# The down projection of a ConvFFN as seven block products in place of eight

## The chip, the core and the metric

The kernel runs on one core of a Trainium2 chip. The metric is device time in microseconds (us). The kernel before takes 1240.32 us, the median of three runs (1239.63 to 1242.1).

## What is computed

One inference step of a decoder layer: a pooling mixer and a Mamba-2 mixer (first 700 us, not touched), their merge, and a ConvFFN over 512 prompt tokens, 64 sample tokens and 16 meta tokens. The change lies in the last lines:

```python
hn2 = rmsnorm(x, norm2_w)
up, ffn_new = causal_dwconv(hn2 @ w_up, ffn_buf, ffn_conv_w, ffn_conv_b)
x = x + (silu(up[..., :D_FF]) * up[..., D_FF:]) @ w_down    # D_MODEL 1024, D_FF 2816
```

After it come a last rmsnorm and the outputs. All data are float32.

## The kernel before, in words

Features lie on the 128 partitions, tokens on the free axis. D_FF is 22 blocks of 128 (gate blocks, j = 0 to 21), D_MODEL 8 blocks (m = 0 to 7). The down projection works on 576 tokens, in two halves of 288.

**A product in three matmuls.** Each float32 operand is split into a high part (a copy in the `F32R` type) and a low part (the rest). `mm3` (lines 117 to 121) multiplies low weight by high activation, high by high, and high weight by low activation, so one block product costs three matmuls, each with its own weight load.

**Units.** A `Unit` (lines 125 to 173) is one output block. `split` takes raw weights from `load_w` (lines 87 to 103: a DMA on SyncE's queue into one of two `wr` buffers, at most two blocks remembered) and splits them: ScalarE copies the high part (line 113), VectorE subtracts for the low part (line 114), into one of two buffers `wh` and `wl`. `product` issues the matmuls, `finish` calls the unit's `post`. `run` (lines 175 to 196) goes through a list of units and splits two units ahead: after unit i's product it splits unit i+2, whose `wh` and `wl` are those that unit i has just read. Outside a block scheduled by hand at the start, the framework orders each engine's instructions ahead of time, and may take a later one that is ready before an earlier one that waits.

**Up projection.** `ff_units` gives a gate unit and a value unit for each j, 48 matmuls each. Both posts call `ffn_conv` (lines 1105 to 1122): VectorE takes the result out of PSUM with three multiplications by the norm (lines 1110 to 1112), ScalarE and VectorE convolve (1118, 1120). `gate_post` applies tanh and a VectorE step (1132, 1133). `val_post` multiplies gate by value (1143), then ScalarE and GpSimd split the product (1147, 1148).

**Down projection.** `down_units` (line 1215) makes one unit per m: first over gate blocks 0 to 11, in two pieces of 6, with 72 matmuls a unit, then, after the other up units, over 12 to 21 with 60 a unit. `down_post` (line 1173) adds the PSUM result to the running sum `x2`. In the last stretch `out_block` (lines 1179 to 1190) transposes a finished block on TensorE, with a square and sum on ScalarE (1189) and a multiplication on VectorE (1190) per tile, and `out_half` (1194 to 1213) scales and stores.

**Buffers.** PSUM has 3 banks under `mm_tile` and 5 under `px_tile`. The pools that matter are `slot` (9), `big` (20), `ext` (3), `acc` (3) and `tmp` (3).

## Time and profile before

| | us |
|---|---|
| median of three runs | 1240.32 |
| the profiled execution | 1240.06 |
| its span, first to last instruction | 1238.3 |
| TensorE matmuls busy | 1215.4 (9148 instructions) |
| VectorE busy | 781.2 |
| ScalarE busy | 557.0 |
| GpSimd busy | 166.4 |

The profile is of one execution. Busy time counts an instruction from its start to its end; matmuls overlap one another, so a busy TensorE is read from the distance of their starts. In the rows PE is TensorE, PEld its weight loads, DVE VectorE, ACT ScalarE, POOL GpSimd, SP SyncE; L114 is line 114. An operand `mm` or `px` lies in PSUM, all others in SBUF.

### The profile page before, as it was taken

How to read it: one execution, taken by the hardware profiler on the slowest of the kernel's cores; microseconds unless marked ns; L12 is line 12 of the kernel's file. 1: busy time of each engine (PE TensorE's matmuls, PEld its weight loads, DVE VectorE, ACT ScalarE, POOL GpSimd, SP SyncE). 2: the span in 40 equal slices, each digit the busy share in tenths (PEclk: the TensorE clock that was granted, in tenths of full speed). 3: DMA queues.
4: the chain of work that ended last, by engine and by line, in shares of the span. 5: the costliest groups of instructions: out<-in, count | busy, mean ns of one | idle time of the engine just before them, and what ended most of it. 6: DMA issues, size and time to landing. Idle time of an engine off the chain costs nothing.

```text
span 1238.3 us, 22581 instructions
## 1 busy us (share of the span) xinstructions
PE 1215.4 (98%) x9148; PEld 1175.7 (95%) x9148; DVE 781.2 (63%) x1372; ACT 557.0 (45%) x1164; POOL 166.4 (13%) x325
## 2 busy tenths in 40 slices
PE   8999999999999999999999999999999999999996
...
PEclk9999999999999999999999999999999999999999
...
GB/s 186 109 76 125 116 89 179 195 179 47 188 83 150 146 120 174 166 128 175 155 146 100 154 149 76 69 69 103 100 71 64 91 86 103 68 69 81 114 75 77
DMA packets 174456, 143.99 MB, mean 116 GB/s; under 512 B 11630, under 2 KB 163854, under 8 KB 174345
## 3 DMA queue, kind: packets, MB, share of 16 engines
...
q10 hardware_dynamic: 384, 0.16, 0.0%
...
## 4 chain that ended last, share of the span: by engine, by line
PE 88%; DMA 4%; DVE 3%; ACT 3%; issue 1%; SPq 1%; ACTq 0%; DVEq 0%
PE mm L119 26%; PE mm L121 26%; PE mm L120 26%; DMA t<-in_state_ssm_dram 3%; PE px L742 1%; PE px L764 1%; PE px L773 1%; DMA t<-in_x_prompt_dram 1%; DVE acc L642 1%; PE px L119 1%; ACT t L852 1%; ACT t L714 1%; PE px L121 1%; PE px L120 1%; PE px L800 1%
## 5 line engine op out<-in xcount | busy, mean ns | idle before, releaser
L119 PE MATMUL mm<-s,wl 128*128 128x288 f32 (+5 forms) x2528 | 757.1, 299 | 1.4 <-ACT s L297 0.9
L120 PE MATMUL mm<-s,wh 128*128 128x288 f32 (+5 forms) x2528 | 752.4, 298 | 0.0
L121 PE MATMUL mm<-s,wh 128*128 128x288 f32 (+5 forms) x2272 | 678.1, 298 | 0.0
L119 PEld LDWEIGHTS mm<-s,wl 128*128 128x128 f32 (+1 forms) x2528 | 476.6, 189 | 10.0 <-issue 6.3
L120 PEld LDWEIGHTS mm<-s,wh 128*128 128x128 f32 (+1 forms) x2528 | 476.6, 189 | 2.7 <-issue 2.4
L121 PEld LDWEIGHTS mm<-s,wh 128*128 128x128 f32 (+1 forms) x2272 | 427.7, 188 | 3.8 <-issue 3.4
L114 DVE TENSOR_TENSOR wl<-wr,wh 128x1024 fp32r<-128x1024 f32 (+2 forms) x165 | 199.3, 1208 | 175.6 <-ACT wh L113 175.1
L113 ACT ACTIVATE wh<-wr 128x1024 fp32r<-128x1024 f32 (+2 forms) x165 | 170.5, 1033 | 233.5 <-PE mm L121 185.5
L121 PE MATMUL mm<-t,wh 128*128 128x290 f32 (+1 forms) x256 | 76.0, 297 | 0.0
L1120 DVE SCALAR_TENSOR_TENSOR acc<-ext,ffT,acc 128x592 f32<-128x592 f32 x88 | 74.2, 844 | 1.7 <-ACT acc L1118 0.2
L642 DVE SCALAR_TENSOR_TENSOR acc<-ext,scT,acc 128x616 f32<-128x616 f32 x72 | 64.0, 889 | 0.8 <-ACT acc L640 0.2
L714 ACT ACTIVATE t<-t,TK 128x128 f32<-128x128 f32 (+1 forms) x160 | 48.5, 384 | 19.4 <-DVE t L712 19.0
L915 POOL TENSOR_TENSOR sqs<-sqs,acc 128x578 f32<-128x578 f32 x19 | 33.4, 1758 | 132.8 <-ACT acc L914 103.3
L121 PEld LDWEIGHTS mm<-t,wh 128*128 128x128 f32 x256 | 48.2, 188 | 0.0
L852 ACT ACTIVATE t<-t,spr 128x128 f32<-128x128 f32 x128 | 40.9, 393 | 12.6 <-PE px L800 12.4
L1147 ACT ACTIVATE s<-ext 128x512 fp32r<-128x512 f32 (+1 forms) x44 | 17.1, 436 | 64.3 <-DVE ext L1143 64.3
L1111 DVE TENSOR_TENSOR ext<-mm,t 128x224 f32<-128x224 f32 x43 | 16.8, 391 | 40.9 <-PE mm L121 40.8
L1148 POOL TENSOR_TENSOR s<-ext,s 128x512 fp32r<-128x512 f32 (+1 forms) x44 | 37.3, 868 | 34.8 <-ACT s L1147 34.8
L1173 DVE TENSOR_TENSOR t<-t,mm 128x288 f32<-128x288 f32 (+2 forms) x30 | 13.6, 452 | 44.5 <-PE mm L121 44.2
L783 POOL TENSOR_TENSOR s<-s,tmp 128x256 f32<-128x256 f32 (+1 forms) x32 | 30.2, 962 | 81.6 <-DVE tmp L777 81.6
L1118 ACT ACTIVATE acc<-ext,ffT 128x592 f32<-128x592 f32 x44 | 38.2, 870 | 1.6 <-DVE ext L1112 1.6
L1114 POOL COPY t<-ext 128x18 f32<-128x18 f32 x44 | 11.4, 259 | 202.6 <-DVE ext L1112 202.5
(290 smaller groups left out, 1274.4 us busy)
## 6 DMA issues: line engine op xcount, KB each, us to landing
...
```

The source lines that it names most:

```text
L113: S.activation(wh[:, :kb, :n], wr, AF.Copy)
L114: V.tensor_tensor(wl[:, :kb, :n], wr, f(wh[:, :kb, :n]), ALU.subtract)
L119: PE.matmul(o, wl[:, k, :m], hi[:, a:b], start=first, stop=False)
L120: PE.matmul(o, wh[:, k, :m], hi[:, a:b], start=False, stop=False)
L121: PE.matmul(o, wh[:, k, :m], lo[:, a:b], start=False, stop=last)
L642: V.scalar_tensor_tensor(acc[:, 0:616], ext[:, k:k + 616], scT[:, kb, 24 + k:25 + k], acc[:, 0:616], op0=ALU.mult, op1=ALU.add)
L714: S.activation(seg[:q, h, :q], seg[:q, h, :q], AF.Exp, scale=-1.0, bias=sums_[:, h:h + 1])
L852: S.activation(v[:, b], v[:, b], AF.Copy, scale=elS[:, 4 * u + 2 * i + b, 4 * g + j:4 * g + j + 1])
L915: G.tensor_tensor(sums[key], sums[key], t[:, :NA], ALU.add)
L1118: S.activation(acc[:, 0:w], ext[:, 0:w], AF.Identity, scale=ffT[:, kb, 16:17], bias=ffT[:, kb, 19:20])
L1120: V.scalar_tensor_tensor(acc[:, 0:w], ext[:, k:k + w], ffT[:, kb, 16 + k:17 + k], acc[:, 0:w], op0=ALU.mult, op1=ALU.add)
L1148: G.tensor_tensor(l, a, f(h), ALU.subtract)
```

## The change

Weights and activations are cut into 2 by 2 blocks: pairs of gate blocks (p = j // 2) against the two blocks of 128 outputs of a column pair (mp) and the two token halves. Seven products of sums and differences replace the eight block products. `Parts` forms the weight sums with four GpSimd additions for each mp and phase; `val_post` forms the activation sums and splits them; `Two` is a unit of two products, each of 3n matmuls of 288 columns for n pairs of gate blocks, and `seven_post` distributes each result to the running sums. A set of seven has eleven VectorE additions and one ScalarE copy behind it.

The order becomes: up units of j 0 to 7, the gate unit of 8, four sets over p 0 to 3, the other up units to j 15, with the gate unit of 16 ahead of four sets over p 4 to 7, the up units to 21, then one set over p 8 and 9, two plain units over blocks 20 and 21, two sets over p 8 to 10, and two plain units (m 6 and 7) over blocks 16 to 21. The output blocks 0 to 3 come between the last sets, 4 and 5 after the first half of m 6. The tile that holds the norm, `rs2`, moves from a `slot` to the tile `sqs`; that hunk is left out here, and empty lines too.

```diff
@@ -171,6 +171,80 @@
             else:
                 self.post(self.pss)
             due[:0] = [fn() for fn in now]
+    SEVEN = (("S3", "T3"), ("A11", "B11"), ("S2", "N2"), ("S1", "N1"), ("A22", "T4"), ("S4", "B22"), ("A12", "B21"))
+    class Parts:
+        def __init__(self, key, nxt):
+            self.key, self.nxt, self.of = key, nxt, None
+        def get(self, name):
+            if self.of is None:
+                wr, n = load_w(*self.key), self.key[2]
+                a11, a12 = wr[:, 0:n:2, 0:128], wr[:, 1:n:2, 0:128]
+                a21, a22 = wr[:, 0:n:2, 128:256], wr[:, 1:n:2, 128:256]
+                s1, s2, s4 = (tmp_tile((128, 4, 128))[:, :n // 2, :] for _ in range(3))
+                G.tensor_tensor(s1, a21, a22, ALU.add)
+                G.tensor_tensor(a21, a11, a21, ALU.add)
+                G.tensor_tensor(s2, s1, a11, ALU.add)
+                G.tensor_tensor(s4, s2, a12, ALU.add)
+                self.of = dict(A11=a11, A12=a12, A22=a22, S1=s1, S2=s2, S3=a21, S4=s4)
+                if self.nxt:
+                    load_w(*self.nxt)
+            return self.of[name]
+    class Two(Unit):
+        def __init__(self, prods):
+            Unit.__init__(self, None, 0, None, None, None, None)
+            self.prods = prods
+        def split(self):
+            if self.ws is None:
+                self.ws = []
+                wh = wp.tile([128, 2, 4, 128], F32R, tag="wh", bufs=WBUFS, name=nm("wh"))
+                wl = wp.tile([128, 2, 4, 128], F32R, tag="wl", bufs=WBUFS, name=nm("wl"))
+                for i, (parts, name, *_) in enumerate(self.prods):
+                    src = parts.get(name)
+                    n = src.shape[1]
+                    S.activation(wh[:, i, :n], src, AF.Copy)
+                    V.tensor_tensor(wl[:, i, :n], src, f(wh[:, i, :n]), ALU.subtract)
+                    self.ws.append(((wh[:, i], wl[:, i]), n))
+        def product(self, halves=None, piece=None):
+            for (_, _, acts, post), (w, n) in zip(self.prods, self.ws):
+                ps = px_tile()
+                for k in range(n):
+                    act = acts(k)
+                    n2 = act[0].shape[1]
+                    mm3(ps[:, :n2], w, k, 128, act, 0, n2, k == 0, k == n - 1)
+                post(ps)
+        def finish(self):
+            for fn in due:
+                fn()
+            due.clear()
+            now = pend[:]
+            pend.clear()
+            due[:0] = [fn() for fn in now]
+    def seven_units(src, k0, kb, mps, acts, post, after=None):
+        keys = [(src, k0, kb, ((256 * mp, 256),)) for mp in mps]
+        prods = []
+        for i, (mp, key) in enumerate(zip(mps, keys)):
+            parts = Parts(key, keys[i + 1] if i + 1 < len(keys) else after)
+            prods += [(parts, w, lambda k, x=x: acts(k)[x], lambda ps, mp=mp, w=w: post(mp, w, ps)) for w, x in SEVEN]
+        return [Two(prods[i:i + 2]) for i in range(0, len(prods), 2)]
     def run(seq, nxt_units=()):
...
     gates = {}
-    gh, gl = [], []
     def gate_post(j, pss):
         ext, acc, w = ffn_conv(j, pss)
@@ -1133,19 +1208,69 @@
         V.scalar_tensor_tensor(ext[:, 0:w], ext[:, 0:w], 1.0, acc[:, 0:w], op0=ALU.add, op1=ALU.mult)
         gates[j] = ext
+    NH = NY // 2
+    gB, quad = {}, {}
+    def split_g(hi, lo, src, eng):
+        S.activation(hi, src, AF.Copy)
+        eng.tensor_tensor(lo, src, f(hi), ALU.subtract)
     def val_post(j, pss):
-        if j % 2 == 0:
-            gh.extend(pairs(2, F32R))
-            gl.extend(pairs(2, F32R))
         _, acc, w = ffn_conv(NF + j, pss)
-        t = gates.pop(j)
-        for a, b in zip(parts(t), parts(acc)):
-            V.tensor_tensor(a, a, b, ALU.mult)
-        hi, lo = blk(gh, j)[:, :NY], blk(gl, j)[:, :NY]
-        for a, h, l in zip(parts(t), (hi[:, 0:NP], hi[:, NP:].rearrange("p (b j) -> p b j", b=NB)),
-                           (lo[:, 0:NP], lo[:, NP:].rearrange("p (b j) -> p b j", b=NB))):
-            S.activation(h, a, AF.Copy)
-            G.tensor_tensor(l, a, f(h), ALU.subtract)
+        t, p, e = gates.pop(j), j // 2, j % 2
+        if e == 0:
+            quad[p] = slot([128, 4, NH])
+        qd = quad[p]
+        g = qd[:, 2 * e:2 * e + 2].rearrange("p h t -> p (h t)")
+        for o, a, b in zip((g[:, 0:NP], g[:, NP:].rearrange("p (b j) -> p b j", b=NB)), parts(t), parts(acc)):
+            V.tensor_tensor(o, a, b, ALU.mult)
+        lastp = p >= 8
+        if e == 0:
+            if lastp:
+                gB[p] = [big([128, 4, NH], F32R) for _ in range(4)]
+                split_g(gB[p][0][:, 0:2], gB[p][1][:, 0:2], qd[:, 0:2], G)
+            else:
+                new = slot if p % 4 == 3 else big
+                gB[p] = [new([128, 4, NH], F32R), new([128, 4, NH], F32R), big([128, 4, NH], F32R),
+                         gB[p - 1][3] if p % 2 else big([128, 4, NH], F32R)]
+                split_g(gB[p][2][:, 0], gB[p][2][:, 2], qd[:, 0], G)
+            return
+        del quad[p]
+        n1, n2 = t[:, 0:NH], t[:, NH:2 * NH]
+        t3, t4 = (acc[:, 0:NH], acc[:, NH:2 * NH]) if lastp else (qd[:, 1], acc[:, 0:NH])
+        o = 2 if lastp else 0
+        if lastp:
+            split_g(gB[p][0][:, 2:4], gB[p][1][:, 2:4], qd[:, 2:4], G)
+        else:
+            split_g(gB[p][0][:, 0:2], gB[p][1][:, 0:2], qd[:, 2:4], G)
+        V.tensor_tensor(n1, qd[:, 0], qd[:, 1], ALU.subtract)
+        V.scalar_tensor_tensor(n2, n1, -1.0, qd[:, 3], op0=ALU.mult, op1=ALU.subtract)
+        V.tensor_tensor(t3, qd[:, 3], qd[:, 1], ALU.subtract)
+        V.scalar_tensor_tensor(t4, n2, -1.0, qd[:, 2], op0=ALU.mult, op1=ALU.subtract)
+        ns = t[:, 0:2 * NH].rearrange("p (h t) -> p h t", h=2)
+        if lastp:
+            split_g(gB[p][2][:, 0:2], gB[p][3][:, 0:2], ns, V)
+            split_g(gB[p][2][:, 2:4], gB[p][3][:, 2:4], acc[:, 0:2 * NH].rearrange("p (h t) -> p h t", h=2), V)
+        else:
+            split_g(gB[p][0][:, 2:4], gB[p][1][:, 2:4], ns, V)
+            split_g(gB[p][2][:, 1], gB[p][2][:, 3], t3, V)
+            i = 2 * (p % 2)
+            split_g(gB[p][3][:, i], gB[p][3][:, i + 1], t4, V)
+    def g_ops(p):
+        a, b, c, d = gB[p]
+        if p >= 8:
+            at = dict(B11=(a, b, 0), B21=(a, b, 2), B22=(a, b, 3), N1=(c, d, 0), N2=(c, d, 1), T3=(c, d, 2), T4=(c, d, 3))
+            return {k: (h[:, i], l[:, i]) for k, (h, l, i) in at.items()}
+        i = 2 * (p % 2)
+        return dict(B21=(a[:, 0], b[:, 0]), B22=(a[:, 1], b[:, 1]), N1=(a[:, 2], b[:, 2]), N2=(a[:, 3], b[:, 3]),
+                    B11=(c[:, 0], c[:, 2]), T3=(c[:, 1], c[:, 3]), T4=(d[:, i], d[:, i + 1]))
+    def g_blk(j):
+        a, b = (x.rearrange("p (e h) t -> p e (h t)", e=2)[:, j % 2] for x in gB[j // 2][0:2])
+        return a, b
     def ff_units(j0, nj):
         out = []
@@ -1185,7 +1310,7 @@
         for i, (t, n) in enumerate(TILES[h]):
             ps = px_tile()[:n, :128]
             PE.transpose(ps, v[:, NMETA + t:NMETA + t + n], ident)
-            junk = tmp_tile()
+            junk = ext_tile()
             S.activation(junk[:n, :128], ps, AF.Square, accum_out=ssq[:n, 3 * h + i, m:m + 1])
             V.tensor_tensor(yts[h][i][:n, ms], ps, fwb[0][:n, ms], ALU.mult)
@@ -1212,28 +1337,66 @@
             if q < n:
                 DMA.dma_start(out=o_ys.rearrange("b j d -> (b j) d"), in_=y[q:n, :])
-    def down_units(j0, kbs, halves):
-        return mat_units(w_dn_m, j0, kbs, 1, lambda: [(blk(gh, j0 + k), blk(gl, j0 + k)) for k in range(sum(kbs))], halves,
-                         lambda m, pss: down_post(m, halves, pss))
-
-    up = ff_units(0, 12)
+    held = {}
+    def seven_post(mp, w, ps):
+        def to(c, src, op):
+            o = blk(x2, 2 * mp + c // 2)[:, NMETA + NH * (c % 2):NMETA + NH * (c % 2) + NH]
+            V.tensor_tensor(o, o, src, op)
+        p = ps[:, :NH]
+        if w == "A11":
+            u = held["u"] = acc_tile()[:, :NH]
+            S.activation(u, p, AF.Copy)
+            to(0, p, ALU.add)
+        elif w == "S2":
+            u = held["u"]
+            V.tensor_tensor(u, u, p, ALU.add)
+            to(2, u, ALU.subtract)
+        elif w == "S1":
+            u = held.pop("u")
+            V.tensor_tensor(u, u, p, ALU.add)
+            to(1, u, ALU.add)
+            to(3, u, ALU.subtract)
+        elif w == "S3":
+            to(2, p, ALU.subtract)
+            to(3, p, ALU.subtract)
+        else:
+            c = {"A22": 2, "S4": 1, "A12": 0}[w]
+            to(c, p, ALU.subtract if c == 2 else ALU.add)
+    def down_sevens(p0, np_, mps, after=None):
+        return seven_units(w_dn_m, 2 * p0, 2 * np_, mps, lambda k: g_ops(p0 + k), seven_post, after)
+    def down_units(j0, kb, ms, halves):
+        return [Unit((w_dn_m, j0, kb, ((256 * (m // 2), 256),)), 128 * (m % 2), [kb], lambda: [g_blk(j0 + k) for k in range(kb)],
+                     halves, lambda pss, m=m: down_post(m, halves, pss)) for m in ms]
+    up = ff_units(0, 8)
     x_turn(0)
     run(o_units, up)
     x2s += [(blk(x2h, k), blk(x2l, k)) for k in range(KD)]
     pend.append(x2_norm)
     up[0].late, up[1].new, up[0].k_outer = True, px_tile, True
-    down0 = down_units(0, [6, 6], GHALF)
-    last = down_units(12, [8, 2], LAST)
-    last[0].mate, last[1].mates, last[1].new = last[1], True, px_tile
-    seq = up + down0 + ff_units(12, 10) + [out_begin, last[0]]
-    for m in range(1, 6):
-        seq += [last[m], *([ff_states] if m == 2 else []), lambda m=m: out_block(0, m - 1), lambda m=m: out_block(1, m - 1)]
-    run(seq, last[6:])
+    up2, up3 = ff_units(8, 8), ff_units(16, 6)
+    seq = up + up2[:1] + down_sevens(0, 4, range(4)) + up2[1:] + up3[:1] + down_sevens(4, 4, range(4)) + up3[1:] + [out_begin]
+    late = down_sevens(8, 2, [0]) + down_units(20, 2, [0, 1], GHALF)
+    for mp in range(1, 3):
+        late += down_sevens(8, 3, [mp])
+    last = down_units(16, 6, [6, 7], LAST)
+    for i, x in enumerate(late):
+        seq.append(x)
+        if i == 6:
+            seq.append(ff_states)
+        if i >= 8:
+            for m in {8: (0,), 9: (1,), 12: (2,), 13: (3,)}.get(i, ()):
+                seq += [lambda m=m: out_block(0, m), lambda m=m: out_block(1, m)]
+    run(seq, last)
     S.activation(eps4[:, 1:2], ssq[:, 0, 0:1], AF.Sqrt)
-    last[7].split()
     for h in range(2):
         for m in (6, 7):
-            u = last[m]
+            u = last[m - 6]
             u.product(LAST[h:h + 1])
             down_post(m, LAST[h:h + 1], u.pss[h:])
             if m == 7:
@@ -1241,8 +1404,9 @@
                 out_block(h, 7)
                 out_half(h)
             elif h == 0:
-                out_block(0, 5)
-                out_block(1, 5)
+                for k in (4, 5):
+                    out_block(0, k)
+                    out_block(1, k)
 _INS = ['x_prompt', 'x_sample', 'state_pool', 'state_conv', 'state_ssm', 'state_ffn', 'meta_tokens', 'norm1_w', 'w_in',
```

## Rows read from the trace of the kernel before

**Rows 1.** The page: its first part (busy time, share of the span, instructions), two lines of its slices (busy tenths of TensorE and its granted clock in tenths, 40 equal slices) and the head of the chain that ended last.

```profile
PE 1215.4 (98%) x9148; PEld 1175.7 (95%) x9148; DVE 781.2 (63%) x1372; ACT 557.0 (45%) x1164; POOL 166.4 (13%) x325
...
PE   8999999999999999999999999999999999999996
...
PEclk9999999999999999999999999999999999999999
...
PE 88%; DMA 4%; DVE 3%; ACT 3%; issue 1%; SPq 1%; ACTq 0%; DVEq 0%
```

**Rows 2.** The busy times by stage: two thirds of the first up-projection stretch, the first down projection (12 gate blocks), the last down projection (10 gate blocks), and the end. Columns: the stretch in us, its length, then busy us and instructions of PE, PEld, DVE, ACT and POOL, the granted clock, the DMA share and GB/s.

```profile
860.00:954.00 94.00, 94.00 (x709) 94.00 (x708) 66.04 (x110) 37.81 (x52) 18.39 (x46) 1.00 0.26 85
954.00:1035.00 81.00, 81.00 (x611) 81.00 (x610) 27.35 (x39) 16.27 (x20) 3.34 (x5) 1.00 0.29 85
1172.00:1228.00 56.00, 56.00 (x428) 55.08 (x427) 24.54 (x70) 21.07 (x93) 0.00 (x0) 1.00 0.24 71
1228.00:1239.00 11.00, 1.04 (x8) 0.56 (x6) 3.31 (x13) 2.79 (x11) 0.00 (x0) 0.78 0.43 129
```

**Rows 3.** The timeline of TensorE inside the first down projection; eleven matmuls of 288 columns, the first and the last shown. Columns: start in us, duration in us.

```profile
999.83 0.29 PE L120 MATMUL mm<-s,wh 128*128 128x288 f32 x1
...
1001.15 0.30 PE L121 MATMUL mm<-s,wh 128*128 128x288 f32 x1
```

**Rows 4.** The groups by line and shape from 880 us to the end. After the count stand busy us and mean ns of one, then the idle time before them and what ended it.

```profile
L114 DVE TENSOR_TENSOR wl<-wr,wh 128x1024 fp32r<-128x1024 f32 x39 | 47.8, 1225 | 22.6 <-ACT wh L113 22.4
L113 ACT ACTIVATE wh<-wr 128x1024 fp32r<-128x1024 f32 x38 | 40.3, 1060 | 60.9 <-PE mm L121 57.8 <-PE px L121 3.1
...
L1148 POOL TENSOR_TENSOR s<-ext,s 128x512 fp32r<-128x512 f32 x17 | 22.0, 1292 | 27.2 <-ACT s L1147 27.2
...
L1143 DVE TENSOR_TENSOR ext<-ext,acc 128x512 f32<-128x512 f32 x17 | 11.6, 683 | 0.1
...
L1147 ACT ACTIVATE s<-ext 128x512 fp32r<-128x512 f32 x17 | 10.7, 632 | 52.0 <-DVE ext L1143 52.0
...
L1173 DVE TENSOR_TENSOR t<-t,mm 128x288 f32<-128x288 f32 x16 | 7.3, 454 | 19.2 <-PE mm L121 19.0
```

**Rows 5.** The timeline of VectorE through one value unit and into the next unit (start us, duration us).

```profile
865.86 0.39 DVE L1111 TENSOR_TENSOR ext<-mm,t 128x224 f32<-128x224 f32 x1 [0.82 <-PE mm L121]
866.16 0.21 DVE L1112 TENSOR_TENSOR ext<-mm,t 128x64 f32<-128x64 f32 x1
866.95 1.23 DVE L114 TENSOR_TENSOR wl<-wr,wh 128x1024 fp32r<-128x1024 f32 x1 [0.57 <-ACT wh L113]
868.09 1.70 DVE L1120 SCALAR_TENSOR_TENSOR acc<-ext,ffT,acc 128x592 f32<-128x592 f32 x2
869.71 0.45 DVE L1110 TENSOR_TENSOR ext<-mm,t 128x290 f32<-128x290 f32 x1
870.08 0.82 DVE L1143 TENSOR_TENSOR ext<-ext,acc 128x512 f32<-128x512 f32 x2
872.24 0.39 DVE L1111 TENSOR_TENSOR ext<-mm,t 128x224 f32<-128x224 f32 x1 [1.34 <-PE mm L121]
```

**Rows 6.** The timeline of VectorE at two places where GpSimd works beside it, about 255 us and about 1152 us (start us, duration us).

```profile
255.54 1.22 DVE L114 TENSOR_TENSOR wl<-wr,wh 128x1024 fp32r<-128x1024 f32 x1
...
257.83 0.41 DVE L853 TENSOR_TENSOR t<-t,px 128x256 f32<-128x256 f32 x1
...
258.76 0.41 DVE L853 TENSOR_TENSOR t<-t,px 128x256 f32<-128x256 f32 x1
...
1152.74 1.16 DVE L114 TENSOR_TENSOR s<-wr,s 128x256 fp32r<-128x256 f32 x1 [1.01 <-ACT s L113]
...
1154.26 0.41 DVE L114 TENSOR_TENSOR s<-wr,s 128x256 fp32r<-128x256 f32 x1
```

**Rows 7.** The timeline of GpSimd at the same two places (start us, duration us, both instructions of a row together).

```profile
255.71 2.79 POOL L783 TENSOR_TENSOR s<-s,tmp 128x256 f32<-128x256 f32 x2 [7.23 <-DVE tmp L777]
...
1152.34 1.74 POOL L1148 TENSOR_TENSOR s<-ext,s 128x512 fp32r<-128x512 f32 x2 [1.36 <-ACT s L1147]
```

**Rows 8.** The timeline of SyncE's queue where one block of w_up, 1 MB, is fetched (start us, duration us).

```profile
861.82 0.37 SPq L95 DMA_DIRECT2D wr<-in_w_up_dram  x1
```

**Rows 9.** The busy times by stage around that fetch; columns as in rows 2.

```profile
861.80:867.00 5.20, 5.20 (x42) 5.20 (x41) 3.29 (x7) 1.84 (x3) 0.22 (x1) 1.00 0.62 205
867.00:868.20 1.20, 1.20 (x12) 1.20 (x11) 1.20 (x2) 0.69 (x1) 0.00 (x0) 1.00 0.00 0
```

**Rows 10.** The timeline of VectorE for the two `out_block` calls of one output block, five tiles (start us, duration us).

```profile
1194.39 0.41 DVE L1173 TENSOR_TENSOR t<-t,mm 128x256 f32<-128x256 f32 x1
1194.72 1.07 DVE L1190 TENSOR_TENSOR s<-px,s 128x128 f32<-128x128 f32 x5
```

**Rows 11.** The timeline of TensorE around the five transposes of one output block (start us, duration us).

```profile
1201.86 0.71 PE L1187 MATMUL px<-ident,t 128*128 128x128 f32 x5
1202.33 0.39 PE L119 MATMUL mm<-s,wl 128*128 128x320 f32 x1
```

14 lines of the change are left out of this document (8 added, 6 removed).

## The prediction

> **What bounds the kernel now.** I read the page first, then the stages, then single instructions. On the page [rows 1] TensorE is busy for 98% of the span, every slice but the first and last is full, the granted clock stays at its upper level (2.4 GHz), and the chain that ended last is 88% TensorE. The stages [rows 2] say the same where the change lies: in both down projections TensorE is busy for the whole stretch. A busy TensorE need not be at its pace, so I take the distance of starts: eleven starts of 288 columns lie 1.32 us apart from first to last [rows 3], 0.132 us each; over the whole first down projection it is 81 us by 611 matmuls, 0.1326 us. So time goes down only with the number of matmuls. The same rows show the reserve: VectorE works 27.4 of 81 us there and GpSimd 3.3, but in the up projection VectorE already works 66.0 of 94 us, 70%. The end, from 1228 us on, is 11 us of short steps and output that the change does not touch.
>
> **What is removed.** Before, the down projection has 12 x 3 x 2 x 8 = 576 and 10 x 3 x 2 x 8 = 480 matmuls, 1056 in all. After: two phases of 4 sets x 7 products x 4 pairs x 3 = 336; then 42 (one set over two pairs), 24 (two plain units), 126 (two sets over three pairs) and 72 (two plain units): 936. The 120 that go are worth 120 x 0.1326 = **15.9 us**. That is the whole gain, since everything else is added work.
>
> **What a set costs beside TensorE.** I use start distances, which are shorter than durations. On VectorE two 592-wide steps and the following start are 1.62 us apart, a 1024-wide one takes 1.14, a 290-wide one from PSUM 0.37 [rows 5], a 256-wide one 0.33 [rows 10]; between them a 512-wide one is about 0.60, a 384-wide one 0.47. A set over four pairs has 84 matmuls, 11.1 us. VectorE has 7 low-part subtractions of 512 (4.2 us) and 11 additions of 288 (4.1): 8.3 us. ScalarE has 7 copies of 512 at 0.63 [rows 4] and one of 288: under 5 us, hidden. GpSimd has four additions of 512 at 1.29 [rows 4]: 5.1 us, done ahead for the next set. If a set's sums ran only when its first unit is split, two of them, a copy and a subtraction (3.9 us) would still fit into the two units, 6.4 us, by which splits run ahead.
>
> But the two engines are not independent. GpSimd's 512-wide addition starts at 1152.34 [rows 7]; VectorE's subtraction of 256 that starts at 1152.74 takes 1.16 us, and the same one at 1154.26 only 0.41 [rows 6]. At 255.71 two GpSimd additions of only 256 take 2.79 us while VectorE has 1024-wide work of the same kind. What has a PSUM operand is spared: L853 takes 0.41 us both beside GpSimd's additions and right after them [rows 6]. So in a set the instructions with two SBUF inputs, 4.2 + 3 x 0.37 = 5.3 us on VectorE, stand in one line with GpSimd's 5.1: 10.4 of 11.1 us. VectorE itself needs between 8.3 us (GpSimd fits into its gaps) and 13.4 (each addition holds it up in full). The truth should be nearer the middle, since eight PSUM additions, 2.9 us, can run beside GpSimd: 8.3 + 3.2 = 11.5, or 0.4 us a set over TensorE. Eight sets: **+3 us**, bounds 0 and (13.4 - 11.1) x 8 = 18. A little lag is free: a unit's first subtraction is ready 1.45 us after the buffers come free and is due after 3.2.
>
> The page GPSIMD Engine Reference (section Engine selection) of the Trainium skill speaks against this choice: two-input elementwise work belongs on VectorE, as GpSimd is about twice as slow. Here it is 1292 ns against 683 [rows 4], so the trace agrees on the ratio. By that rule the sums would go to VectorE at 4 x 0.60 us, a set would need 10.7 us, and the +3 would be 0.
>
> **Up projection.** Each two gate blocks add four VectorE sums of 288 and about 1.4 us of subtractions, 2.9 us, and 1 us on ScalarE; GpSimd gets less. Their four units last 25.5 us, in which VectorE has 30% idle [rows 2], 7.6 us; one value unit shows 1.34 us of it in one piece [rows 5]. I cost it at nothing. Without that cover it would be up to 2.9 us for each of 11 pairs.
>
> **Entries.** Each of the first two phases starts one gate unit (6.4 us) after its last value unit. From that unit's end VectorE and ScalarE need about 7.6 us to the last pair's T3 (0.45 out of PSUM, 1.2 for the split ahead, 1.6 convolution, 0.8 multiplication, then three sums, ScalarE's copies and the subtraction); the first product needs it at its fourth pair, 6.4 + 1.2 = 7.6. No slack: **+2 us** for both, bounds 0 and 5.
>
> **The third phase** is the tight one. Set 0 (5.6 us) and the two plain units (3.2) give 8.8 us of TensorE. VectorE has in that time the post of the last value unit (5.6: 2.8 as now, 1.5 sums, 1.3 subtractions), set 0's splits (1.7) and additions (4.1), the plain units (2.1) and the next set's first splits (1.9): 15.4 us, of which about 2 can come later. That is 4.5 us too much; GpSimd's split of the last value and the next sums (another 5 us) come on top where they hold VectorE up, and buffers that let TensorE run ahead come off. I take **+4.5**, bounds 1 and 8. Set 1 needs 7.4 plus two output blocks of 1.07 [rows 10], 9.5 us, against 8.35 + 2 x 0.47 [rows 11] = 9.3, with GpSimd beside it: **+1**, bounds 0 and 3. Set 2 has no sums behind it: 0. At the end five more tiles stand ahead of the last units, 1.1 us on VectorE: **+0.5**, bounds 0 and 1.
>
> **Transfers.** w_down is fetched in 1 MB pieces, and two pieces of w_up are fetched twice, as only two blocks are remembered. A piece that is issued at 861.82 [rows 8] is in by 867.0, after which the DMA engines are idle [rows 9]: 5.2 us. SyncE's queue holds only these here. A set needs a new piece every 11.1 us; at the re-entry into the up units the buffer comes free about 10 us before its split: nothing. Without that cover, up to 5.2 us at each of two places. Moving `rs2` adds only a wait on a reader that is long done: nothing.
>
> **The sum**: -15.9 + 3 + 2 + 4.5 + 1 + 0.5 = -4.9 us. The profiled execution took 1240.06 (its span 1238.3), 0.3 below the median of 1240.32: 1240.06 - 4.9 = **1235.2 us**.
>
> **Rivals.** *All hidden.* VectorE's additions slip behind what TensorE needs (five PSUM banks allow four products of delay), so stalls stay under 5 us. For it: the shared line is 94% full, not over. Against it: the third phase, where the work does not fit at all. 1240.06 - 15.9 + 2 = 1226 us; 1224 to 1229.
>
> *The lock decides; slower.* In the eight full sets each GpSimd addition stops VectorE for its whole length, in front of a subtraction that TensorE waits for. Price: (13.4 - 11.1) x 8 = 18 in place of 3: 1235.2 + 15 = 1250 us. It decides, and the sign turns, from (15.9 - 8) / 8 = 1 us a set over TensorE on, 12.1 us of VectorE. For it: the 1.16 us against 0.41 [rows 6]. Against it: the PSUM additions, and GpSimd idle for half of each set. The Trainium skill (SBUF — State Buffer, section Who interferes with whom) describes this as an exclusive lock that blocks the other fully; both rows of VectorE bear that out.
>
> *It cancels.* Stalls of 13.4 to 18.4 us; the third phase at its upper bounds (12) with the entries does it: 1237.6 to 1242.5 us.
>
> *It does less than it says*, that is, fewer matmuls go: excluded by the count above, which follows from the loops.
>
> **Chances.** Partial gain (1229 to 1237.6) 0.48, all hidden 0.20, cancels 0.13, lock 0.19. A measurement here can tell about 0.2%, 2.5 us. Faster: 0.68; same 0.13; slower 0.19. The range takes in most of the first case's edge and part of the lock: 1226 to 1245; about 0.07 lies below and 0.13 above. Without the lock the forecast's own range is 1229 to 1237.6.
>
> **What would show it.** 120 matmuls fewer in lines 119 to 121's groups, at an unchanged 0.13 us. In the full sets VectorE busy for 75 to 100%, its subtractions at times over 1 us where GpSimd's sums run, and gaps of TensorE that end on `wl`: few and under 1 us by the forecast, 2 us per set by the lock, none if all is hidden. TensorE idle for some 5 us between the last value unit and set 1. GpSimd busier by some 40 us (51 of sums, less in the splits). Wrong it would be if TensorE waited for `wr` or for GpSimd, if the matmuls' pace changed, or if the up projection itself became slower.

## The result, and the profile after

The change made the kernel slower: 1256.97 us (1253.97 to 1258.92) against 1239.97 (1239.18 to 1242.1) for the kernel before on the same chip, ratio 1.0132 [1.0108, 1.0156]. That is 22 us above the forecast and outside its range. The profiled execution took 1253.97 us, its span is 1252.3. The page of the kernel after, the lines that answer to [rows 1]:

```profile
PE 1209.6 (97%) x9028; PEld 1164.7 (93%) x9028; DVE 900.8 (72%) x1592; ACT 591.2 (47%) x1232; POOL 243.0 (19%) x347
...
PE   8999999999999999999999999999989999899976
...
PEclk8999999999999999999999999999999999999989
...
PE 81%; DVE 11%; ACT 3%; DMA 3%; issue 1%; SPq 1%; POOL 0%; ACTq 0%; DVEq 0%; POOLq 0%
```

The 120 matmuls are gone (9148 to 9028), but TensorE's row now has an 8 in the 30th and the 35th slice, where the first two phases' sets begin (the **entries** below), and a 7 in the 39th, where the third phase runs; the chain of work that ended last runs for 11% through VectorE in place of 3%. VectorE has 120 us more, GpSimd 77 more. The busy times by stage show where TensorE stands still; columns as in [rows 2]:

```profile
810.00:907.00 97.00, 97.00 (x733) 97.00 (x733) 82.93 (x140) 43.90 (x59) 30.53 (x41) 1.00 0.29 93
907.00:921.00 14.00, 10.62 (x65) 9.92 (x64) 13.84 (x25) 7.37 (x13) 8.28 (x8) 0.88 0.00 1
912.00:916.00 4.00, 3.93 (x18) 3.93 (x19) 4.00 (x8) 2.20 (x4) 3.11 (x4) 0.58 0.00 0
921.00:957.00 36.00, 34.27 (x255) 33.62 (x254) 32.95 (x57) 12.65 (x23) 13.35 (x9) 1.00 0.27 89
...
1188.00:1194.50 6.50, 2.10 (x13) 1.86 (x12) 6.50 (x13) 3.06 (x8) 1.56 (x1) 0.85 0.00 0
1194.50:1200.00 5.50, 5.50 (x27) 5.50 (x27) 5.32 (x14) 0.69 (x3) 0.00 (x0) 0.55 0.44 142
1200.00:1206.00 6.00, 3.55 (x27) 3.32 (x26) 4.06 (x8) 1.99 (x4) 4.60 (x5) 1.00 0.40 132
```

The up projection (first row) is still full. At the entry to the first phase's sets (second row; the third shows four microseconds of it) VectorE works 13.84 of 14 us and TensorE 10.62; in the three sets that follow the loss is small; at the start of the third phase VectorE is busy without a break for 6.5 us, and TensorE for 2.1. Next, the timeline of TensorE: the idle times of the first entry, the pace just ahead of the large gap (first and last of 24 matmuls), and behind it (first and last of 23), then the later idle times. Columns: start, duration, and in brackets the idle time with what ended it.

```profile
910.13 0.40 PE L119 MATMUL px<-s,wl 128*128 128x288 f32 x1 [0.74 <-ACT s L1215]
912.07 0.40 PE L121 MATMUL px<-s,wh 128*128 128x288 f32 x1 [1.41 <-DVE s L1216]
920.02 0.40 PE L119 MATMUL px<-s,wl 128*128 128x288 f32 x1 [1.24 <-DVE wl L220]
...
1185.79 0.29 PE L119 MATMUL px<-s,wl 128*128 128x288 f32 x1
...
1188.84 0.29 PE L121 MATMUL px<-s,wh 128*128 128x288 f32 x1
1193.54 0.61 PE L119 MATMUL px<-s,wl 128*128 128x288 f32 x1 [4.40 <-DVE wl L220]
1193.95 0.44 PE L120 MATMUL px<-s,wh 128*128 128x288 f32 x1
...
1199.23 0.38 PE L121 MATMUL mm<-s,s 128*128 128x288 f32 x1
...
1204.45 0.40 PE L119 MATMUL px<-s,wl 128*128 128x288 f32 x1 [2.45 <-DVE wl L220]
...
1215.18 0.40 PE L119 MATMUL px<-s,wl 128*128 128x288 f32 x1 [0.98 <-DVE s L1315]
1218.79 0.40 PE L119 MATMUL px<-s,wl 128*128 128x288 f32 x1 [1.27 <-DVE s L1315]
1228.15 0.41 PE L119 MATMUL mm<-s,wl 128*128 128x320 f32 x1 [1.05 <-DVE wl L114]
```

The pace is unchanged where nothing is missing: 23 distances in 3.05 us, 0.133 each, as in [rows 3]. Behind the 4.40 us the distance is 0.24 (22 in 5.28 us): the granted clock of 1194.5 to 1200 is 0.55, so for most of it the lower level of 1.2 GHz; in the 6.50 us ahead of it TensorE had been busy for 2.10.

I add up the gaps of TensorE from the last matmul of the norm ahead of the up projection to the last instruction. That stretch, called **norm to end** below, is 430.8 us before and 447.0 after, +16.2. A **gap** is a distance of two starts over 0.4 us, less the 0.133 that it would have taken; the one ahead of the last output block's transposes, 0.4 to 0.7 us in every kernel here, is not counted. Before there is no other; after there are 24.6 us of them, and 7.3 us more in shorter ones and at the lower clock: -15.9 + 24.6 + 7.3 = +16.0. The gaps by place: entries 3.9 and 5.4 (within the first set's first two units and ahead of its third), in the full sets behind that 4.0, third phase 11.3.

VectorE's side of an entry shows why. First VectorE, then GpSimd, where the first set's sums begin:

```profile
896.57 1.22 DVE L114 TENSOR_TENSOR wl<-wr,wh 128x1024 fp32r<-128x1024 f32 x1 [0.57 <-ACT wh L113]
897.71 3.64 DVE L1196 SCALAR_TENSOR_TENSOR acc<-ext,ffT,acc 128x592 f32<-128x592 f32 x2
901.28 0.45 DVE L1186 TENSOR_TENSOR ext<-mm,sqs 128x290 f32<-128x290 f32 x1
...
903.50 1.95 DVE L220 TENSOR_TENSOR wl<-wr,wh 128x512 fp32r<-128x512 f32 x2
905.37 1.69 DVE L1196 SCALAR_TENSOR_TENSOR acc<-ext,ffT,acc 128x592 f32<-128x592 f32 x2
```

```profile
897.21 1.72 POOL L195 TENSOR_TENSOR tmp<-wr 128x512 f32<-128x512 f32 x1 [0.86 <-DMA wr<-in_w_down_dram]
899.01 1.71 POOL L196 TENSOR_TENSOR wr<-wr 128x512 f32<-128x512 f32 x1
900.68 1.83 POOL L197 TENSOR_TENSOR tmp<-tmp,wr 128x512 f32<-128x512 f32 x1
902.59 1.71 POOL L198 TENSOR_TENSOR tmp<-tmp,wr 128x512 f32<-128x512 f32 x1
```

Two 592-wide steps of L1196 take 3.64 us beside GpSimd's sums and 1.69 at 905.37, when they are over ([rows 5] have 1.70). The multiplication with a PSUM operand (L1186) takes 0.45 beside the sums, as in [rows 5]. GpSimd's additions take 1.7 to 1.8 us in place of 1.29 [rows 4]: both engines are slowed. The first set's sums stand beside the convolution of the last gate unit ahead of the entry (L1196 at 897.71; the one at 905.37 is its value unit's). They end at 904.30, long before their products; what the entry waits for at 910.13 and 912.07 are the splits of gate times value (L1215, L1216 in `val_post`), which stand behind both convolutions and come late.

### The profile page after: what moved, and what is told of

It reads as the page before. It is cut to its first block, busy times and chain, and to the rows that moved or that the text cites. A ratio compares the mean times of both kernels' runs of the same rounds, so it can differ in the third digit from the quotient of the medians.

```text
span 1252.3 us, 22734 instructions
## 1 busy us (share of the span) xinstructions
PE 1209.6 (97%) x9028; PEld 1164.7 (93%) x9028; DVE 900.8 (72%) x1592; ACT 591.2 (47%) x1232; POOL 243.0 (19%) x347
## 3 DMA queue, kind: packets, MB, share of 16 engines
q8 instruction: 71, 1.16, 0.4%
## 4 chain that ended last, share of the span: by engine, by line
PE 81%; DVE 11%; ACT 3%; DMA 3%; issue 1%; SPq 1%; POOL 0%; ACTq 0%; DVEq 0%; POOLq 0%
PE mm L119 22%; PE mm L121 21%; PE mm L120 21%; PE px L119 2%; DVE wl L220 2%; PE px L121 2%; PE px L120 2%; DVE acc L1196 2%; DMA t<-in_state_ssm_dram 2%; PE px L816 1%; PE px L838 1%; PE px L874 1%; PE px L847 1%; DVE wl L114 1%; DVE t L1346 1%
## 5 line engine op out<-in xcount | busy, mean ns | idle before, releaser
L119 PE MATMUL mm<-s,wl 128*128 128x290 f32 (+4 forms) x2248 | 673.5, 300 | 3.0 <-DVE wl L114 2.5
L120 PE MATMUL mm<-s,wh 128*128 128x290 f32 (+4 forms) x2248 | 669.4, 298 | 0.0
L121 PE MATMUL mm<-s,wh 128*128 128x290 f32 (+3 forms) x1992 | 594.8, 299 | 0.0
L119 PEld LDWEIGHTS mm<-s,wl 128*128 128x128 f32 (+1 forms) x2248 | 423.3, 188 | 11.7 <-issue 6.3
L120 PEld LDWEIGHTS mm<-s,wh 128*128 128x128 f32 (+1 forms) x2248 | 423.3, 188 | 2.8 <-issue 2.4
L121 PEld LDWEIGHTS mm<-s,wh 128*128 128x128 f32 (+1 forms) x1992 | 374.5, 188 | 3.9 <-issue 3.4
L114 DVE TENSOR_TENSOR wl<-wr,wh 128x1024 fp32r<-128x1024 f32 (+2 forms) x143 | 176.2, 1232 | 135.6 <-ACT wh L113 135.2
L119 PE MATMUL px<-s,wl 128*128 128x288 f32 (+3 forms) x280 | 86.5, 309 | 18.0 <-DVE wl L220 14.2
L121 PE MATMUL px<-s,wh 128*128 128x288 f32 (+3 forms) x280 | 84.9, 303 | 2.8 <-DVE s L1216 2.8
L120 PE MATMUL px<-s,wh 128*128 128x288 f32 (+3 forms) x280 | 84.7, 302 | 0.0
L1196 DVE SCALAR_TENSOR_TENSOR acc<-ext,ffT,acc 128x592 f32<-128x592 f32 x88 | 81.2, 924 | 1.3 <-ACT acc L1194 0.2
L119 PEld LDWEIGHTS px<-s,wl 128*128 128x128 f32 (+1 forms) x280 | 53.6, 191 | 21.6 <-DVE wl L220 16.4
L121 PEld LDWEIGHTS px<-s,wh 128*128 128x128 f32 (+1 forms) x280 | 53.7, 192 | 3.8 <-DVE s L1216 3.3
L120 PEld LDWEIGHTS px<-s,wh 128*128 128x128 f32 (+1 forms) x280 | 53.8, 192 | 0.3
L926 ACT ACTIVATE t<-t,spr 128x128 f32<-128x128 f32 x128 | 40.9, 393 | 13.4 <-PE px L874 13.3
```

Of the source, the lines that this page charges most:

```text
L114: V.tensor_tensor(wl[:, :kb, :n], wr, f(wh[:, :kb, :n]), ALU.subtract)
L119: PE.matmul(o, wl[:, k, :m], hi[:, a:b], start=first, stop=False)
L120: PE.matmul(o, wh[:, k, :m], hi[:, a:b], start=False, stop=False)
L121: PE.matmul(o, wh[:, k, :m], lo[:, a:b], start=False, stop=last)
L926: S.activation(v[:, b], v[:, b], AF.Copy, scale=elS[:, 4 * u + 2 * i + b, 4 * g + j:4 * g + j + 1])
L1196: V.scalar_tensor_tensor(acc[:, 0:w], ext[:, k:k + w], ffT[:, kb, 16 + k:17 + k], acc[:, 0:w], op0=ALU.mult, op1=ALU.add)
```

## The experiments

All times in one table; the ratio is to the kernel before, run beside each on the same chip. The kernel before took 1239.97 us beside the change, 1240.3 beside e1 to e4, 1240.28 beside e5 to e8, 1239.46 beside e9 and e10, 1240.69 beside e11 and e12 and 1239.8 beside e13 and e14; so a difference between runs of two of these groups can hold up to 1.2 us that the kernel before shows as well. Norm to end and gaps are those of the profiled run.

| run | us (range) | ratio [95%] | norm to end | gaps |
|---|---|---|---|---|
| before | 1239.97 (1239.18 to 1242.1) | | 430.8 | 0 |
| the change | 1256.97 (1253.97 to 1258.92) | 1.0132 [1.0108, 1.0156] | 447.0 | 24.6 |
| e1_sums_on_vector | 1247.57 (1246.07 to 1249.31) | 1.0047 [1.0032, 1.0062] | 438.8 | 18.0 |
| e2_no_sums | 1240.15 (1239.37 to 1244.15) | 1.0000 [0.9985, 1.0015] | 432.4 | 13.2 |
| e3_plain_third_phase | 1246.13 (1244.85 to 1249.29) | 1.0043 [1.0026, 1.0061] | 436.1 | 13.3 |
| e4_order | 1252.73 (1249.38 to 1256.95) | 1.0090 [1.0063, 1.0117] | 443.1 | 22.7 |
| e5_two_gates_ahead | 1254.26 (1251.03 to 1256.73) | 1.0102 [1.0086, 1.0118] | 444.3 | 23.8 |
| e10_other_banks | 1251.35 (1250.36 to 1251.79) | 1.0094 [1.0076, 1.0111] | 443.4 | 20.6 |
| e6_three_mended | 1235.08 (1233.78 to 1236.28) | 0.9949 [0.9937, 0.9962] | 425.6 | 6.0 |
| e7_mended_gpsimd_sums | 1244.58 (1241.51 to 1246.15) | 1.0029 [1.0019, 1.0039] | 432.8 | 13.3 |
| e8_dead_additions | 1261.28 (1258.3 to 1263.08) | 1.0154 [1.0137, 1.0171] | 449.7 | 23.2 |
| e11_dead_on_constants | 1243.78 (1240.98 to 1246.79) | 1.0026 [1.0015, 1.0038] | 426.0 | 6.1 |
| e12_dead_copies | 1235.51 (1234.26 to 1236.48) | 0.9957 [0.9942, 0.9972] | 426.0 | 6.1 |
| e13_dead_in_the_sets | 1247.17 (1246.62 to 1248.58) | 1.0060 [1.0045, 1.0075] | 437.9 | 15.8 |
| e14_copies_in_the_sets | 1237.25 (1234.42 to 1238.52) | 0.9974 [0.9963, 0.9985] | 428.4 | 8.5 |
| e9_late_post | 1235.65 (1233.22 to 1238.37) | 0.9965 [0.9952, 0.9978] | 426.0 | 6.8 |
| e9_late_and_order | 1233.2 (1230.46 to 1235.55) | 0.9946 [0.9929, 0.9962] | 423.5 | 4.1 |
| e9_order_alone | 1232.31 (1231.13 to 1233.02) | 0.9938 [0.9924, 0.9951] | 423.7 | 4.3 |

**e1_sums_on_vector**, the four sums on the other engine:

```diff
-                G.tensor_tensor(s1, a21, a22, ALU.add)
+                V.tensor_tensor(s1, a21, a22, ALU.add)
```

(and so the other three).

> The four weight sums of every set go from GpSimd to VectorE, nothing else. The changed kernel took 1257 us, with TensorE idle for 25 us in gaps over 0.4 us. Lock theory (GpSimd's additions stop VectorE's two-SBUF-input instructions for their whole length): VectorE gets 2.4 us of work more for each full set but loses the hold-ups; its 288-wide and 512-wide instructions keep to 0.45 and 0.68 us, the gaps fall to some 12 us, 1244 to 1250 us. Load theory (VectorE simply has too much to do beside TensorE, lock or not): it gets worse, 10 sets by about 1 to 2 us each, 1265 us or more. Latency theory (the sums come too late for the splits): 1252 to 1257, since a VectorE sum is shorter but queues behind the additions.

9.4 us faster than the change. The gaps at the entries fall from 9.3 to 6.1 us and those in the sets behind from 4.0 to 1.2, both of 0.6 at the start of a second set; the third phase keeps 10.8 of its 11.3. VectorE has 44 instructions more than in the change and is busy for no longer:

```profile
PE 1208.4 (97%) x9028; PEld 1164.4 (93%) x9028; DVE 899.8 (72%) x1636; ACT 591.9 (48%) x1232; POOL 178.3 (14%) x303
```

So with the sums on GpSimd VectorE saved nothing at all: it worked as long on fewer instructions, and part of that longer work stood in the steps that an entry waits for.

**e2_no_sums** leaves the sums out; the computation is changed (four of the products use a block of the weights in place of a sum).

```diff
-                G.tensor_tensor(s1, a21, a22, ALU.add)
...
+                s1, s2, s4 = a21, a11, a12
```

> The four weight sums of every set are left out (an unsummed weight block stands in each one's place), so no GpSimd work belongs to the sets any more; TensorE, VectorE and ScalarE do what they did. Lock theory: the price of the sums is most of the idle time, 15 to 20 us come back, 1237 to 1242 us. Load theory: 5 us at most, 1252 us or more. Latency theory: the sums' own place in the chain goes too, 1240 to 1248, but then VectorE's long instructions (1.3 to 1.8 us for a 288- or 512-wide one) would not be what ends the gaps in the changed kernel.

1240.2, the lock theory's number: the sums cost 16.8 us on GpSimd and 7.4 on VectorE. VectorE has the same 1592 instructions of the same shapes as in the change, yet it is busy for 22.8 us less:

```profile
PE 1204.2 (97%) x9028; PEld 1161.8 (94%) x9028; DVE 878.0 (71%) x1592; ACT 591.3 (48%) x1232; POOL 178.2 (14%) x303
```

But without any sums the change still gains nothing: 13.2 us of gaps are left, 4.3 at the entries and 9.0 in the third phase, the first of them 4.4 us from start to start, with VectorE busy throughout (columns as above, the stretch of that gap):

```profile
1177.80:1182.20 4.40, 0.27 (x3) 0.03 (x2) 4.40 (x9) 1.78 (x3) 1.57 (x1) 0.76 0.00 0
```

GpSimd holds VectorE up here too, with a split that the kernel before had as well: the low part of the last value unit. VectorE's rows at the first entry and ahead of the third phase's gap, then GpSimd's (lines of this kernel stand four lower than in the change):

```profile
907.44 0.46 DVE L1243 SCALAR_TENSOR_TENSOR ext<-ext,t 128x288 f32<-128x288 f32 x1
...
908.19 1.70 DVE L1245 SCALAR_TENSOR_TENSOR acc<-ext,t 128x288 f32<-128x288 f32 x1
...
1180.51 1.62 DVE L216 TENSOR_TENSOR wl<-wr,wh 128x256 fp32r<-128x256 f32 x1
...
1182.43 0.41 DVE L216 TENSOR_TENSOR wl<-wr,wh 128x256 fp32r<-128x256 f32 x1
```

```profile
907.84 1.72 POOL L1212 TENSOR_TENSOR t<-t,t 128x576 fp32r<-128x576 f32 x1 [1.54 <-ACT t L1211]
...
1180.28 1.57 POOL L1212 TENSOR_TENSOR s<-t,s 128x576 fp32r<-128x576 f32 x1 [4.44 <-ACT s L1211]
```

Each time an instruction of VectorE takes 1.2 us more than its like, and TensorE then waits for it or for a later one of VectorE; the first gap of that entry is 1.1 us, so the hold-up alone covers it. No run moved this split, so its price is read from these rows alone.

**e3_plain_third_phase** keeps the sevens in the first two phases and computes blocks 16 to 21 as before, with 24 matmuls (3.2 us) more.

```diff
-    late = down_sevens(8, 2, [0]) + down_units(20, 2, [0, 1], GHALF)
-    for mp in range(1, 3):
-        late += down_sevens(8, 3, [mp])
...
+    last = down_units(16, 6, range(8), LAST)
```

> Sevens in the first two phases only; gate blocks 16 to 21 go through plain units with the output blocks placed as in the kernel before. 24 matmuls more than the changed kernel (3.2 us); TensorE's idle time from the last value unit on (about 13 us in gaps over 0.4 us, 2.7 us of matmuls at the lower granted clock) goes. If the third phase's set costs what its gaps say: 1257 + 3 - 14 = 1246 us. If that stretch is limited by the output blocks and the end instead, and the gaps only move: 1257 to 1260 us. In both the first two phases keep their gaps of some 13 us.

10.8 us faster in spite of the added matmuls. The third phase's gaps shrink from 11.3 to 1.0 us; the sevens there cost about 14 us (10.8 and the 3.2 of the added matmuls) to save 3.2.

**e4_order**: which product comes first.

```diff
-    SEVEN = (("S3", "T3"), ("A11", "B11"), ("S2", "N2"), ("S1", "N1"), ("A22", "T4"), ("S4", "B22"), ("A12", "B21"))
+    SEVEN = (("A11", "B11"), ("A12", "B21"), ("S3", "T3"), ("S2", "N2"), ("S1", "N1"), ("A22", "T4"), ("S4", "B22"))
```

> The seven products are taken in another order: the two that need no sums (A11 with B11, A12 with B21) first, then S3, S2, S1, A22, S4. Operand theory of the entries (the first products wait for T3, N2 and their weight sums): the two entries' gaps, some 9.4 us, shrink to 3, and 1250 to 1252 us come out. Lock and load theories: VectorE is behind by the same amount, so the gaps move by a product or two; 1255 to 1259 us.

1252.7, between the two theories; its interval touches both. Inconclusive by itself.

**e5_two_gates_ahead**: a second gate unit ahead of each of the first two phases.

```diff
-    seq = up + up2[:1] + down_sevens(0, 4, range(4)) + up2[1:] + up3[:1] + down_sevens(4, 4, range(4)) + up3[1:] + [out_begin]
+    a2, a3 = [up2[0], up2[2]], [up3[0], up3[2]]
+    seq = up + a2 + down_sevens(0, 4, range(4)) + [up2[1]] + up2[3:] + a3 + down_sevens(4, 4, range(4)) + [up3[1]] + up3[3:] + [out_begin]
```

> The changed kernel with one thing moved: ahead of each of the first two phases stand two gate units (j 8 and 9, 16 and 17) in place of one, so that the last pair's operands have 12.8 us, not 6.4, to become ready. The sums stay on GpSimd. Entry theory (the entries' 9.4 us of gaps are the last value unit's chain on VectorE and ScalarE, too late by some 2 to 4 us): the gaps after 900 us and after 1060 us fall to 2 us together, 1248 to 1250 us. Load theory (VectorE is behind for good, and the second gate unit brings 4.7 us of its work for 6.4 us of TensorE): the gaps move into the sets, 1254 us or more.

The entry theory fell: the gaps moved deeper into the first set. As distances of starts, the first phase had 1.03 and 1.71 us inside the first product and 1.53 ahead of the third unit; now each phase has 1.08 ahead of the second unit and 3.37 ahead of the third. More TensorE work ahead did not help while VectorE was held up.

**e10_other_banks**: the small sets' products in the other PSUM tiles.

```diff
-                ps = px_tile()
+                ps = mm_tile() if n < 4 else px_tile()
```

> Edit: the change as it is (1257.0 us), but the products of the third phase's sets over fewer than four pairs take their PSUM tile from the banks of the other matmuls (three of them) in place of the five that out_block's tiles fill. Bank theory (the gaps of 1.3, 1.6 and 1.4 us at the last sets come from out_block's tiles holding all five banks until VectorE's L1315 has read them): they go, 1252.5 to 1254. Load theory (VectorE and ScalarE do not keep up in the third phase, whichever bank is written): the gaps move, 1256 to 1259, or more since three banks run less far ahead than five.

5.6 us faster, 5.1 without what the kernel before shows as well and 3.6 in norm to end of the profiled runs, where the bank theory said 3 to 4.5. No product waits on L1315 any more, so it holds for those two gaps (2.3 us); the 1.05 us on L114 was another wait, which the expectation had counted in. The rest does not come from those two waits: the order on TensorE moved with the edit, the 4.40 us fell apart into idle times of at most 1.34 us, and the 2.45 us shrank to 1.33.

**e6_three_mended**: the three diffs of e1, e3 and e5 in one kernel.

> Sums on VectorE, a plain third phase and two gate units ahead of the first two phases, together. The 96 matmuls that are left out are worth 12.7 us. If the three causes (lock, third phase, entries) are all there is: TensorE idle for under 3 us, 1229 to 1234 us, faster than the kernel before. If VectorE cannot carry sums, splits and additions of a set (10.7 of 11.1 us): gaps of 0.5 to 1 us in most sets, 1236 to 1242 us.

1235.1, 22 us under the change and 0.5% under the kernel before. That lies between the two ranges expected. It has 96 matmuls fewer than before (12.7 us) and 6.0 us of gaps, which stand at the entries, 2.5 us a phase, and not in most sets; 1.0 is in the third phase.

**e7_mended_gpsimd_sums**: e6 with e1's diff taken back, the sums on GpSimd again.

> As the kernel with all three mended, but the sums on GpSimd as in the change. Lock theory: eight sets with GpSimd's 5.1 us in them, VectorE's two-SBUF instructions up to 1.8 us long, 0.5 to 1 us a set: 1236 to 1241 us. If the lock hurt only where the entries were late, it is hidden now: within 2 us of the one with sums on VectorE, or faster than it, since VectorE is spared 19 us of work.

+9.5 us with nothing else changed, about the 9.4 of e1, now without the third phase, and over the 1241 that the lock theory allowed. Both entries have e5's distances of 1.1 and 3.4 us again. VectorE lost 32 additions of 0.68 us, 21.8 us of work, and was busy for 871.8 us in place of 869.4.

**e8_dead_additions**: e6 and, per set, five additions on GpSimd whose result nobody reads.

```diff
+                for _ in range(5):
+                    G.tensor_tensor(TK[:, :, 0:128], a11[:, 0:3], a22[:, 0:3], ALU.add)
```

> As the kernel with all three mended (sums on VectorE), with five GpSimd additions of 384 columns in each set that read two blocks of the raw weights and whose result nobody reads: 4.8 us a set, as much as the sums took there. Nothing waits for them but the next use of the weight buffer, which has some 6 us of room. Lock theory: the same hold-ups on a VectorE that also has the sums, 1240 to 1248 us. Latency theory (GpSimd's sums cost because the splits wait for them): no difference to the kernel without them, within 2 us.

+26.2 us. Nothing waits for their result, so the latency theory falls; but the lock theory's 1240 to 1248 is passed as well. These additions also waited for the fetch of `w_down` and kept its buffer (waits of GpSimd, 900 to 990 us; total, times, longest):

```profile
POOL TK L200 <- DMA wr<-in_w_down_dram: 19.4, 3, 12.2
```

**e11_dead_on_constants** and **e12_dead_copies** were to tell these apart: the dead instructions read a resident table, as additions and as copies.

```diff
-                    G.tensor_tensor(TK[:, :, 0:128], a11[:, 0:3], a22[:, 0:3], ALU.add)
+                    G.tensor_tensor(TK[:, :, 0:128], TK[:, :, 0:128], TK[:, :, 0:128], ALU.add)
```

> Edit: as e8_dead_additions (1261.3 us, 26 over e6_three_mended; VectorE's same 1564 instructions were busy for 893.0 us there in place of 869.4), but the five dead additions of 384 columns read a table that stays in SBUF and not the set's weights, so that they neither wait for the fetch of w_down nor keep its buffer. Lock theory (GpSimd's two-operand work in SBUF holds VectorE up): VectorE's busy time again 15 to 24 us over 869.4, time 1253 to 1263. Buffer theory (e8 lost its time because the weights' buffer came free later and the next fetch with it, and because GpSimd's queue stood at that fetch): VectorE busy within 5 us of 869.4, time 1235 to 1240.

> Edit: as e11_dead_on_constants, but each dead instruction copies the table's 384 columns onto themselves: one SBUF operand in place of two. If any GpSimd work holds VectorE up: VectorE's busy time grows by about as much per microsecond of GpSimd as in e11 (some 0.4), and the time with it, 1245 to 1260. If only two-operand work does: VectorE busy 869 to 874 us, time 1235 to 1239, though GpSimd works 20 to 55 us more.

Both missed their place: with nothing to wait for, the dead instructions were put at 564 to 606 us, ahead of the ConvFFN, so norm to end is e6's in both. They tell nothing of the sets. (e11's 8.7 us arose before the norm, where the dead additions came onto the chain.)

**e13_dead_in_the_sets** and **e14_copies_in_the_sets** tie them to the sets by a 16-column copy:

```diff
+                G.tensor_copy(TK[:, :, 0:16], s4[:, 0:3, 0:16])
                 for _ in range(5):
                     G.tensor_tensor(TK[:, :, 0:128], TK[:, :, 0:128], TK[:, :, 0:128], ALU.add)
```

> Edit: as e11_dead_on_constants, with a 16-column copy from the set's last sum ahead of each five dead additions, so that they run in the sets and not at 564 to 606 us as there; they still read no buffer of the weights and wait for no fetch. Lock theory: VectorE busy 10 to 24 us over the 869.4 us of e6_three_mended, time 1245 to 1262. Buffer theory (e8's loss came from the weights' buffer and the fetch): VectorE busy within 5 us of 869.4, time 1235 to 1239.

> Edit: as e13_dead_in_the_sets, with copies of 384 columns (one SBUF operand, 0.51 us each where nothing disturbs them) in place of the additions (0.83 us). If any GpSimd work holds VectorE up: VectorE's busy time grows by 0.6 of what e13 shows, 1241 to 1252. If only two-operand work does: VectorE busy 869 to 873, time 1235 to 1238.

e13: +12.1 us, VectorE +14.5: the lock theory's numbers, with no buffer of the raw weights held and no fetch waited for. The page of e6, then of e13; VectorE's 1564 instructions are the same:

```profile
PE 1207.0 (98%) x9052; PEld 1163.9 (94%) x9052; DVE 869.4 (70%) x1564; ACT 581.8 (47%) x1206; POOL 174.6 (14%) x303
```

```profile
PE 1210.1 (97%) x9052; PEld 1164.2 (93%) x9052; DVE 883.9 (71%) x1564; ACT 581.9 (47%) x1206; POOL 218.6 (18%) x351
```

Five dead additions at 935.27 to 940.70 us, on GpSimd, and VectorE in that time and just after it (L223 and L1350 here are L220 and L1346 of the change):

```profile
935.27 5.43 POOL L201 TENSOR_TENSOR TK<-TK 128x384 f32<-128x384 f32 x5
```

```profile
935.49 1.16 DVE L223 TENSOR_TENSOR wl<-wr,wh 128x512 fp32r<-128x512 f32 x1
936.57 1.31 DVE L223 TENSOR_TENSOR wl<-tmp,wh 128x512 fp32r<-128x512 f32 x1
937.80 1.17 DVE L1350 TENSOR_TENSOR t<-t,px 128x288 f32<-128x288 f32 x3
...
941.17 0.44 DVE L1350 TENSOR_TENSOR t<-t,px 128x288 f32<-128x288 f32 x1
...
941.90 0.68 DVE L195 TENSOR_TENSOR tmp<-wr 128x512 f32<-128x512 f32 x1
```

The 512-wide instructions take 1.16 to 1.31 us in that stretch and 0.68 after it, while three additions with a PSUM operand take 1.17 together beside GpSimd, 0.39 each, and one after it 0.44. e14's copies cost 2.2 us and VectorE 5.2: the time is the one expected if two-operand work alone holds VectorE up, but VectorE's 874.6 us is over that theory's 873, so copies do so too, by less. Of e8's 26 us, the hold-up alone makes about 12; the other 14 came with the weights' buffer and fetch, or with additions that lasted longer there (a mean of 1436 ns against e13's 1076). Which of these, stays open.

**e9_late_post, e9_late_and_order, e9_order_alone** work on the gaps that e6 has left.

```diff
+    a2[1].late = a3[1].late = True
...
-    SEVEN = (("S3", "T3"), ("A11", "B11"), ("S2", "N2"), ("S1", "N1"), ("A22", "T4"), ("S4", "B22"), ("A12", "B21"))
+    SEVEN = (("A11", "B11"), ("A12", "B21"), ("S4", "B22"), ("S3", "T3"), ("S2", "N2"), ("S1", "N1"), ("A22", "T4"))
```

The first line is e9_late_post, the other edit e9_order_alone.

> Edit: the mended kernel (e6_three_mended: sums on VectorE, third phase plain, two gate units ahead; 1235.1 us) with the multiplication of the second of the two gate units that run ahead put off behind the first set. Post theory (the 0.7, 1.5 and 0.7 us gaps at each of its two entries come from that unit's convolution and multiplication, which stand on VectorE ahead of the first set's subtractions): most of the 5.8 us goes, 1230 to 1232.5. Load theory (the entry's splits are late because VectorE has too much to do there in any order): the gaps move into the set, 1234 to 1237.

> Edit: as e9_late_post, and the order of the seven products is A11, A12, S4, S3, S2, S1, A22. Operand theory (the first products wait for operands that are formed last: A11 and A12 need no sum, and T3 is wanted three products later): 1 to 2 us under e9_late_post, 1229 to 1231. Load theory: within 1 us of e9_late_post.

> Edit: e6_three_mended (1235.1 us) with the order A11, A12, S4, S3, S2, S1, A22 alone. Operand theory: 1 to 3 us faster, 1232 to 1234. Load theory: 1235 to 1236.

The late post gains nothing (distances of 0.7, 1.2 and 1.35 us per phase in place of 0.7, 1.5 and 0.7): the post theory falls. The order gains 2.8 us against e6, 0.8 of which the kernel before shows as well, and 1.9 in norm to end; between e9_late_post and e9_late_and_order, on one chip, it is 2.5. That is the operand theory's number, but only half of its reason is borne out: in e6 TensorE waits at the entries for the weights' low parts, not for T3.

```profile
926.18 0.40 PE L119 MATMUL px<-s,wl 128*128 128x288 f32 x1 [1.23 <-DVE wl L220]
```

This wait ahead of the third unit is gone with the order, which puts two products whose weights need no sum first. Both together are not better than the order alone. e9_order_alone is the fastest kernel: 0.62% under the kernel before and 2% under the change.

## Why the prediction was wrong, step by step

**Removed matmuls, -15.9: right.** 120 fewer, at an unchanged pace.

**Up projection, 0: right.** 97 of 97 us, though VectorE now works 82.93 of them.

**A set beside TensorE, +3: the step that failed.** I took a value between two bounds, on the reason that additions with a PSUM operand can run beside GpSimd, and I priced it in the full sets alone. The 3.2 us of hold-up in it do not follow from that reason: 5.1 less the 2.9 of those additions is 2.2, which would have made the term nothing. In the full sets it came out at 4.0 us, so the 3 is near it by luck. But the sums as a whole cost 16.8 us (e2), 13.8 of the 22 us by which the forecast was short; the other 8 are the entries and the third phase, since e2, without sums, is level with the kernel before where my other terms leave 7.9 us of gain. The 16.8 are made up as follows: 5.0 us more of gaps at the entries, 4.0 in the sets, 2.4 in the third phase, 3.2 in short gaps and at the lower clock, together 14.6 from norm to end; the other 2.2 lie in the part before the norm and in the scatter of runs. GpSimd's sums were "done ahead for the next set", and so the first set's stood beside the entry, where I had found no slack myself and still charged them nothing.

What the sums take of VectorE: in the change GpSimd works 64.8 us more than in e2 and VectorE 22.8 us longer over the same instructions, 0.35 us for each. e13 gives 14.5 for 44.0, 0.33; e8 23.6 for 58.1, 0.41. My figure of 3.2 us per set (of 5.1) was 0.63. So I over-priced the hold-up itself and over-rated the reserve against it: VectorE's 8.3 of 11.1 us holds for a set, not for the 14 us of an entry, and of the 22.8 us that VectorE lost, three quarters (16.8) reached the end.

The Trainium skill (SBUF — State Buffer, section Who interferes with whom) says that a VectorE instruction with two SBUF inputs contends with a GpSimd instruction that reads SBUF, and that one with at most one does not. The rows agree: L223 1.16 to 1.31 against 0.68, L1350 with a PSUM input 0.39 beside GpSimd, and copies, which read SBUF too, hold VectorE up as well (e14). The rule of the Trainium skill's GPSIMD Engine Reference (section Engine selection), by which the prediction's +3 would be 0, pointed the right way; e1 gives 9.4 us of gain, not 3.

**Entries, +2 (0 to 5): too small.** 9.3 us with the sums, 4.3 without. That is inside the bounds without the sums, but I had left GpSimd's split of the last value out of the entry: behind its hold-up of 1.2 us stand 2.1 of the 4.3 us.

**Third phase, +4.5, +1 and 0: mechanism right, size wrong.** VectorE does stand in for the end there (6.50 of 6.50 us), and the gap of 4.4 us arises without any sums (e2), 1.2 of it behind GpSimd's split of the last value, which I had named. I left out what follows from it: behind the gap 22 distances of 0.24 us, 5.28 us in place of 2.93, so 2.4 us more at the lower clock; the two waits on out_block's tiles in the five PSUM banks (0.98 and 1.27 us; e10); and the next term.

**Transfers, 0: wrong at one place.** The buffer came free only at 1196.39, when set 0's last split was over, and the sums stood behind the fetch in series. The chain of waits of the change (start us, us, what):

```profile
1195.89 0.35 DVE wl L220
1196.39 4.17 DMA wr<-in_w_down_dram
...
1200.69 1.02 POOL tmp L195
1201.79 1.25 POOL wr L196
1203.06 0.53 ACT wh L219
1203.61 0.79 DVE wl L220
```

TensorE stood for 2.45 us there. In e2 the same wait for the fetch left a gap of 0.5, so the sums behind the fetch make it matter. I had said "a set needs a new piece every 11.1 us" of sets in which VectorE keeps up.

**The rivals.** "The lock decides" named the right mechanism and side; its 1250 was 7 us short, since it priced the full sets alone and kept the third phase's +4.5. That its price of 18 us lies near the 16.8 of e2 is luck: it had each microsecond of GpSimd's additions stop VectorE for a whole one, where 0.35 was measured, and it looked for the loss in the full sets, where 4.0 us arose. **The range**: all upper bounds of my terms together give 1240.06 - 15.9 + 18 + 5 + 8 + 3 + 1 = 1259.2, which holds the result. I cut it to 1245 as if the terms could not all go up at once; they share one cause, VectorE without reserve, and did.
